# Scores one tile ahead of the softmax behind, and the last two row tiles of the down projection by halves of the tokens

## The chip, the cores and the metric

The kernel runs on one core of one Trainium2 chip. The time is the device time of one launch in microseconds; three runs of the kernel before were taken, and one more under the profiler.

## The reference, cut to what matters

Two layers over 512 tokens of width 1024 in float32. The first layer mixes tokens with a gated delta rule, the second with sliding-window attention; both also attend into 256 memory rows. After each mix comes a projection back to the width, and a feed-forward block. The change touches the attention of the second layer, and the end: the last down projection with the final norm.

```python
def sliding_window_attention(q, k, v, sinks):      # 12 heads of 64, window 128, blocks of 128 queries
    ...
    s = jnp.einsum("bnqhgd,bnkhd->bnhgqk", qb, kw).astype(jnp.float32) * (SWA_DH ** -0.5)
    ...
    m = jnp.maximum(jnp.max(s, axis=-1, keepdims=True), sink)
    p = jnp.exp(s - m)
    p = (p / (jnp.sum(p, axis=-1, keepdims=True) + jnp.exp(sink - m))).astype(v.dtype)
    o = jnp.einsum("bnhgqk,bnkhd->bnqhgd", p, vw)
...
for layer in range(DEPTH):
    ...
    x = x + jnp.concatenate([mix_out, mem_o], axis=-1) @ w_out[layer]
    x = x + swiglu(rms_norm(x, ln_ffn[layer]), w_gate_up[layer], w_down[layer])
    ...
return rms_norm(x, ln_final)
```

`memory_attention` is the same softmax attention without window and sinks, over 256 memory rows, 4 heads of 64.

## The kernel before, in words

Activations lie transposed: features on the 128 partitions, the 512 tokens along the free dimension, eight tiles `x[0..7]` for the width. Every large product is made of three matmuls (`mm3`): weight and activation are split into a high and a low part that TensorE takes at its fast rate, by `split` (ACT makes the high part `whi`, DVE the low part `wlo`), and high x high, high x low, low x high are added in PSUM. A projection (`project`) of one output tile is 8 x 3 = 24 matmuls of 128x512. Weights come by transfers from the SP queue into `wraw` (two buffers), and `whi` and `wlo` have three buffers each.

The program is written with a scheduler that takes the instructions in the order of the text as priority, and puts an instruction of lower priority ahead where its model of the times lets it start earlier. So the order on an engine isn't the order of the text alone. `nosync` adds an edge that only fixes the order of two instructions.

`swa` is the second layer's mixing. Eight attention tiles t: 0 to 5 hold two heads each of the window attention, 6 and 7 the memory heads. `queries(t)` projects tile t into `q` (three buffers) in a PSUM bank of the tag `pj` (two banks), and DVE applies the rotary embedding (`rope`, four operations). `attend(t)` calls `attention`, which does, for one tile of two heads and four blocks n of 128 queries: scores (TensorE, 8 matmuls into the double bank `qk`, twice: blocks 0 and 1, then 2 and 3, with one buffer); the masked maximum (DVE) into `sm`; exponentials with sums (ACT); the reciprocal and the scaling (DVE and ACT in turns); transposes of the probabilities into banks `pt` (two), their copies `pf`; products with the values into the bank `sc`; and the split of the result into `mix[t]`. `attention` serves the first layer's memory heads too. Then `output` projects, over mix tiles 6, 7, 0, 1, 2, 3, 4, 5, for each of eight output tiles.

`ffn` does the feed-forward block in two halves of 11 feature tiles. In the second half of the last layer, `tail` is 7: tiles 0 to 6 of the down projection are done with all 512 tokens, and tile 7 with the first 256 tokens and then the last 256. After each half of tile 7 comes `final`: the sum of squares by two matmuls with a matrix of ones, logarithm and exponential on ACT (`ps`, then a copy to `rstd`), products with the gains on DVE and, for tiles 4 and 5, on POOL, and four output transfers from SP.

Of the kernel before, what the change touches and what calls it, by code (L numbers as in the profile page):

```python
# [9 lines left out]
F32 = mybir.dt.float32  # L10
F32R = mybir.dt.float32r
I32 = mybir.dt.int32
AF = mybir.ActivationFunctionType
ALU = mybir.AluOpType
# [4 lines left out]
P = 128  # L19
T = 512  # L20
D = 1024
KD = D // P
# [63 lines left out]
class Builder:  # L86
# [53 lines left out]
        return self.nc.scalar.activation(out, in_, AF.Square).ins  # L140

    def mm(self, out, lhsT, rhs, start=True, stop=True):
        self.nc.tensor.matmul(out, lhsT, rhs, start=start, stop=stop)  # L143

    def tr(self, out, in_):
        k = in_.shape[0]
        self.nc.tensor.transpose(out, in_, self.ident[:k, :k])  # L147

    def tt(self, eng, out, a, b, op):
        return eng.tensor_tensor(out=out, in0=a, in1=b, op=op).ins  # L150
# [557 lines left out]


    def attention(self, pool, q, kk, vv, m, out, sinks=None):  # L710

        nc = self.nc
        win = sinks is not None
        own = "pt" in self.pbufs
        half = [slice(0, 64), slice(64, P)]
        sm = [self.t(pool, [P, 2, 2, 2 * P], F32, "sm", 4 if own else 2) for _ in range(2)]
        sm = [t[:, n] for t in sm for n in range(2)]
        mx = self.t(pool, [P, 2 * NC], F32, "mx", 2)
        den = self.t(pool, [P, 2 * NC], F32, "den", 2)
        nm = self.t(pool, [P, 2 * NC], F32, "nm", 2)  # L720
        for n0 in range(0, NC, 2):
            if own:
                two = self.bank("qk", [P, 2, 2, 2 * P])
                ps = [two[:, b] for b in range(2)]
            else:
                ps = [self.bank("sc" if n0 else "g", [P, 2, 2 * P]) for _ in range(2)]
            for n in (n0, n0 + 1):
                ks = slice((n - 1) * P if n else 0, (n + 1) * P) if win else slice(0, ML)
                c0 = P if win and n == 0 else 0
                for b in range(2):  # L730
                    self.mm(ps[b][:, n - n0, c0:], q[half[b], n * P:(n + 1) * P], kk[half[b], ks])
            for b in range(2):
                i = b * NC + n0
                if win:
                    for n in (n0, n0 + 1):
                        c0 = 0 if n else P
                        nc.vector.tensor_tensor_reduce(
                            out=sm[n][:, b, c0:], in0=ps[b][:, n - n0, c0:], in1=self.band[:, c0:], scale=1.0,
                            scalar=NEG, op0=ALU.add, op1=ALU.max, accum_out=mx[:, b * NC + n:b * NC + n + 1])
                else:  # L740
                    nc.vector.tensor_reduce(out=mx[:, i:i + 2], in_=ps[b], op=ALU.max, axis=AX.X)  # L741
                    self.ts(nm[:, i:i + 2], mx[:, i:i + 2], -0.125, ALU.mult)
                    for n in (n0, n0 + 1):
                        i = b * NC + n
                        self.fn(sm[n][:, b, :], ps[b][:, n - n0, :], AF.Exp, scale=0.125, bias=nm[:, i:i + 1],
                                accum_out=den[:, i:i + 1])
        if win:
            sk = sinks.unsqueeze(2).to_broadcast([P, 2, NC])
            v4 = lambda ap: ap.rearrange("p (b n) -> p b n", b=2)
            self.stt(v4(mx), v4(mx), 0.125, sk, ALU.mult, ALU.max)  # L750
            self.ts(nm, mx, -1.0, ALU.mult)
            es = self.t(pool, [P, 2 * NC], F32, "es", 2)
            self.tt(nc.vector, v4(es), v4(nm), sk, ALU.add)
            self.fn(es, es, AF.Exp)
            for n in range(NC):
                c0 = 0 if n else P
                for b in range(2):
                    i = b * NC + n
                    self.fn(sm[n][:, b, c0:], sm[n][:, b, c0:], AF.Exp, scale=0.125, bias=nm[:, i:i + 1],
                            accum_out=den[:, i:i + 1])  # L760
            self.tt(nc.vector, den, den, es, ALU.add)
        nc.vector.reciprocal(den, den)
        o = self.bank("sc")
        group = NC if own else 2
        for n in range(NC):
            if n % group == 0:
                pf = {}
            k0 = 1 if win and n == 0 else 0
            p = sm[n][:, :, k0 * P:]
            dn = den.rearrange("p (b n) -> p n b", b=2)[:, n, :]  # L770
            for b in range(2):
                if n % 2:
                    self.copy(p[:, b], p[:, b], scale=dn[:, b:b + 1])
                else:
                    self.ts(p[:, b], p[:, b], dn[:, b:b + 1], ALU.mult)
            pt = self.bank("pt" if own else "g", [P, 2, 2, P])
            for j in range(k0, 2):
                for b in range(2):
                    self.tr(pt[:, j, b, :], sm[n][:, b, j * P:(j + 1) * P])
            pf[n] = self.t(pool, [P, 2, 2, P], F32, "pf", group)  # L780
            if own and n == 2:
                nc.vector.tensor_copy(pf[n][:, k0:], pt[:, k0:])
            else:
                self.copy(pf[n][:, k0:], pt[:, k0:])
            if (n + 1) % group:
                continue
            for n, t in pf.items():
                for j in range(1 if win and n == 0 else 0, 2):
                    for b in range(2):
                        v = vv[n - 1 + j][:, half[b]] if win else vv[j][:, m * P + 64 * b:m * P + 64 * b + 64]  # L790
                        self.mm(o[half[b], n * P:(n + 1) * P], v, t[:, j, b, :], win and n == 0 or j == 0, j == 1)
        self.split(o, *out)


# [16 lines left out]
    def ffn(self, fp, xp, layer, h, apool, rope=False):  # L811
        nc, a = self.nc, self.a
        acc = self.acc
        half = FT // 2
        for f0 in (0, half):
# [16 lines left out]
                if rope and f == 4:  # L832
                    self.rope_tables(fp)
            self.acc = None
            tail = KD - 1 if f0 and layer else KD
            down = lambda m, j, n, **kw: self.weight(a["wdn"][layer, m][:, (f0 + j) * P:(f0 + j + n) * P], **kw)
            for m in range(tail):
                ps = self.bank("pj")
# [6 lines left out]
                    self.acc = self.accumulate(xp, self.acc, self.x[m], m)  # L845
        if tail < KD:

            w = {m: [down(m, j, n, pool=fp if m == KD - 1 and tail < KD - 1 else None) for j, n in ((0, 6), (6, 5))] for m in range(tail, KD)}
            for t in (slice(0, T // 2), slice(T // 2, T)):
                acc = self.acc[:, t]  # L850
                for m in range(tail, KD):
                    ps = self.bank("pj")[:, :T // 2]
                    for k in range(half):
                        self.mm3(ps, w[m][k // 6], k % 6, [x[:, t] for x in acts[k]], k == 0, k == half - 1)
                    x = self.x[m][:, t]
                    self.tt(nc.vector, x, ps, x, ALU.add)
                sq = self.t(fp, [P, T // 2], F32, "sql", 2)
                self.square(sq, x)
                self.final(fp, (acc, sq), t)

    def rstd_from(self, acc, t=slice(0, T)):
        self.use(LN_EXP)
# [50 lines left out]
    def swa(self, sp):  # L913
# [38 lines left out]
            self.copy(vt.rearrange("p c i -> p (c i)"), pt)  # L952
            vv.extend(vt[:, c, :] for c in range(NC))

        def attend(t):
            mix[t] = self.pair(self.bpool)
            if t < 6:
                self.attention(sp, qs[t], kk[0], vv, t, mix[t], sinks[:, t, :])
            else:
                self.attention(sp, qs[t], memK[t - 6], memV, t - 6, mix[t])  # L960

        queries(6)
        queries(7)
        keys()
        values()
        attend(6)
        transpose_values()
        queries(0)
        attend(7)
        for t in range(6):  # L970
            if t < 5:
                queries(t + 1)
            attend(t)
        return [mix[t] for t in range(KD)]

    def final(self, fp, squares, t):

        nc = self.nc
        self.use(LN_EXP)
        ps = self.bank("g")[:, t]  # L980
        for k, sq in enumerate(squares):
            self.mm(ps, self.ones, sq, k == 0, k == len(squares) - 1)
        self.fn(ps, ps, AF.Ln, scale=1.0 / D, bias=self.eps)
        self.fn(ps, ps, AF.Exp, scale=-0.5)
        r = self.rstd[:, t]
        self.copy(r, ps)
        rows = self.a["out"].rearrange("(k p) t -> p k t", p=P)
        for k0 in (4, 0, 2, 6):
            o = self.t(fp, [P, 2, T // 2], F32, f"fin{k0}", 2)
            for k in (k0, k0 + 1):  # L990
                x, y = self.x[k][:, t], o[:, k - k0, :]
                if k0 == 4:
                    self.copy(y, x, scale=self.gain(G_FIN, k))
                    self.tt(nc.gpsimd, y, y, r, ALU.mult)
                else:
                    self.stt(y, x, self.gain(G_FIN, k), ps, ALU.mult, ALU.mult)
            nc.sync.dma_start(rows[:, k0:k0 + 2, t], o)


def layout(i):  # L1000
# [56 lines left out]
```

## Time and profile before

| what | us |
|---|---|
| median of three runs (lowest, highest) | 1206.13 (1206.08, 1208.48) |
| the profiled execution | 1205.06 |
| its span, first to last instruction | 1203.3 |
| the second layer's attention, on the profile's time line | about 697 to 801 |
| the last row tile and the end | 1183.9 to 1203.3 |

The span is that of one execution; the 1.8 us between span and the execution's time lie around the program. The profile has, for each engine, the busy time; groups of equal instructions with their mean duration; the idle time in front of each and what ended it; and the instructions in order of time. PE is TensorE's matmuls, PEld its weight loads, DVE the vector engine, ACT the scalar engine, POOL GpSimd, SP the queue that issues the transfers.

### The profile page before, as it was taken

The numbers are of one execution on the slowest core, as the hardware profiler recorded it, in microseconds if no ns is written. First come the engines' busy times: TensorE is split into PE (matmuls) and PEld (weight loads), VectorE is DVE, ScalarE is ACT, GpSimd is POOL, SyncE is SP. The second block draws the span as 40 slices with busy tenths as digits, with TensorE's granted clock in tenths as the row PEclk, the third lists the DMA queues.
The fourth block names the chain that finished last, engine by engine and source line by source line (L and its number), as shares of the span: only waits on it lengthen the run. The fifth ranks groups of instructions, "written<-read, shape, count | busy, mean of one in ns | idle before, by whom it ended". The sixth has DMA issues, their size and how long they took to land.

```text
span 1203.3 us, 15347 instructions
## 1 busy us (share of the span) xinstructions
PE 1181.1 (98%) x6009; PEld 961.1 (80%) x6009; DVE 620.3 (52%) x1058; ACT 504.2 (42%) x929; POOL 92.5 (8%) x63
## 2 busy tenths in 40 slices
PE   7999999999999999999999999999999999999996
PEld 6888777877888888888888877678888888888885
DVE  5654977668753433343434667755434333444343
ACT  7578672456432322232333456664323222322332
POOL 0210000000011100011100000000111100111100
PEclk9999999999999999999999999999999999999999
DMA  7334352325323223423233411113232234232232
GB/s 297 134 95 130 95 129 79 121 77 162 105 88 105 84 84 96 123 88 105 84 84 97 139 54 42 47 37 122 88 105 88 82 96 120 89 104 89 84 97 81
DMA packets 51037, 121.08 MB, mean 101 GB/s; under 512 B 14300, under 2 KB 17012, under 8 KB 50964
## 3 DMA queue, kind: packets, MB, share of 16 engines
q1 hardware_dynamic: 50964, 120.10, 32.3%
q8 instruction: 47, 0.77, 0.3%
q14 instruction: 26, 0.21, 0.1%
HBM read 113.12 MB, written 6.96 MB: 100 GB/s over the span
## 4 chain that ended last, share of the span: by engine, by line
PE 89%; DVE 6%; ACT 2%; DMA 1%; issue 1%; SPq 0%; DVEq 0%; ACTq 0%
PE pj L143 57%; PE g L143 24%; PE sc L143 6%; DVE wlo L150 1%; PE pt L147 1%; ACT sm L131 1%; PE g L147 1%; DMA wraw<-in_wmk 1%; ACT whi L137 1%; DVE btmp L150 1%; PE qk L143 0%; DVE big L150 0%; DVE mx L741 0%; DMA wraw<-in_win 0%; DMA big<-basein 0%
## 5 line engine op out<-in xcount | busy, mean ns | idle before, releaser
L137 ACT ACTIVATE whi<-wraw 128x1024 fp32r<-128x1024 f32 (+2 forms) x213 | 207.6, 975 | 564.9 <-PE pj L143 366.6
L143 PE MATMUL pj<-h,whi 128*128 128x512 f32 (+1 forms) x972 | 381.6, 393 | 0.1
L143 PE MATMUL pj<-l,whi 128*128 128x512 f32 (+1 forms) x972 | 380.2, 391 | 0.0
L143 PE MATMUL pj<-h,wlo 128*128 128x512 f32 (+1 forms) x972 | 379.4, 391 | 0.0
L150 DVE TENSOR_TENSOR wlo<-wraw,whi 128x1024 fp32r<-128x1024 f32 (+2 forms) x213 | 238.3, 1119 | 147.0 <-ACT whi L137 146.6
L143 PEld LDWEIGHTS pj<-h,whi 128*128 128x128 f32 x972 | 182.5, 188 | 41.0 <-issue 4.2
L143 PEld LDWEIGHTS pj<-l,whi 128*128 128x128 f32 x972 | 182.7, 188 | 38.9 <-issue 2.6
L143 PEld LDWEIGHTS pj<-h,wlo 128*128 128x128 f32 x972 | 182.6, 188 | 38.9 <-issue 2.2
L150 POOL TENSOR_TENSOR fg<-fg,rstd 128x512 f32<-128x512 f32 x44 | 75.5, 1716 | 988.2 <-ACT fg L131 988.2
L143 PE MATMUL g<-h,wlo 128*128 128x512 f32 x380 | 148.0, 389 | 0.0
L143 PE MATMUL g<-l,whi 128*128 128x512 f32 x380 | 148.0, 389 | 0.0
L143 PE MATMUL g<-h,whi 128*128 128x512 f32 x380 | 147.9, 389 | 0.0
L150 DVE TENSOR_TENSOR fu<-g,fg 128x512 f32<-128x512 f32 x44 | 30.4, 691 | 142.7 <-PE g L143 140.0
L150 DVE TENSOR_TENSOR fg<-pj,rstd 128x512 f32<-128x512 f32 x44 | 30.4, 691 | 110.7 <-PE pj L143 110.4
L143 PEld LDWEIGHTS g<-h,wlo 128*128 128x128 f32 x380 | 71.4, 188 | 15.0 <-issue 0.2
L143 PEld LDWEIGHTS g<-h,whi 128*128 128x128 f32 x380 | 71.3, 188 | 14.8
L143 PEld LDWEIGHTS g<-l,whi 128*128 128x128 f32 x380 | 71.3, 188 | 14.8 <-issue 0.2
L150 DVE TENSOR_TENSOR x<-pj,x 128x512 f32<-128x512 f32 (+1 forms) x45 | 30.4, 678 | 68.2 <-PE pj L143 68.2
L131 ACT ACTIVATE fg<-fg 128x512 f32<-128x512 f32 x44 | 27.7, 630 | 1.5 <-DVE fg L150 1.5
L153 DVE SCALAR_TENSOR_TENSOR qv<-pj,gains,qv 128x511 f32<-128x511 f32 (+2 forms) x36 | 26.7, 743 | 1.1 <-ACT qv L137 0.8
L140 ACT ACTIVATE sq<-x 128x512 f32<-128x512 f32 x39 | 24.1, 624 | 6.2 <-DVE x L150 3.9
L137 ACT ACTIVATE h<-x,gains 128x512 fp32r<-128x512 f32 x32 | 22.1, 712 | 5.9 <-DVE x L150 5.9
(301 smaller groups left out, 1198.5 us busy)
## 6 DMA issues: line engine op xcount, KB each, us to landing
wraw<-in_wgu SPq DMA_DIRECT2D x88, 512.0 KB, 3.5
wraw<-in_win SPq DMA_DIRECT2D x26, 512.0 KB, 3.6
wraw<-in_wdn SPq DMA_DIRECT2D x32, 384.0 KB, 3.1
wraw<-in_wdn SPq DMA_DIRECT2D x32, 320.0 KB, 2.9
wraw<-in_wout SPq DMA_DIRECT2D x16, 512.0 KB, 3.5
wraw<-in_wq SPq DMA_DIRECT2D x8, 512.0 KB, 3.5
x<-in_xT SPq DMA_DIRECT2D x4, 512.0 KB, 9.0
wraw<-in_wmv SPq DMA_DIRECT2D x4, 512.0 KB, 9.0
```

Of the source, the lines that this page charges most:

```text
L131: ins = self.nc.scalar.activation(out, in_, func, **kw).ins
L137: self.copied = self.nc.scalar.activation(out, in_, AF.Copy, **kw).ins
L140: return self.nc.scalar.activation(out, in_, AF.Square).ins
L143: self.nc.tensor.matmul(out, lhsT, rhs, start=start, stop=stop)
L147: self.nc.tensor.transpose(out, in_, self.ident[:k, :k])
L150: return eng.tensor_tensor(out=out, in0=a, in1=b, op=op).ins
L153: self.nc.vector.scalar_tensor_tensor(out=out, in0=in0, scalar=scalar, in1=in1, op0=op0, op1=op1)
```

## The change

`attention` is cut in two: `scores` (up to the exponentials of the memory heads, or to the masked maximum of the window heads) and `weigh` (the rest). In `swa` the scores of tile t are written ahead of `weigh` of the tile before it. Two edges are added on TensorE: the first transpose of a tile's probabilities comes after the last score of the tile ahead, and the first value product after the last transpose of its group. The first layer still calls both in a row.

In the last feed-forward block `tail` becomes 6, so tiles 6 and 7 are both done by halves of the tokens, and the weights of tile 7 lie in another pool. The products of `x` with the final gain are made ahead on ACT for tiles 0 to 5, both halves. `final` now ends with two exponentials, one into PSUM and one into SBUF, and `store` multiplies: tiles 0 and 1 on POOL, 2 to 5 on DVE two at a time, 6 and 7 on DVE one at a time. The stores of both halves are written after both halves' matmuls. The diff, without the changes that only return an instruction:

```diff
@@ -708,9 +708,11 @@
 
 
     def attention(self, pool, q, kk, vv, m, out, sinks=None):
+        self.weigh(pool, self.scores(pool, q, kk, sinks is not None), vv, m, out, sinks)
+
+    def scores(self, pool, q, kk, win):
 
         nc = self.nc
-        win = sinks is not None
         own = "pt" in self.pbufs
         half = [slice(0, 64), slice(64, P)]
         sm = [self.t(pool, [P, 2, 2, 2 * P], F32, "sm", 4 if own else 2) for _ in range(2)]
@@ -728,7 +730,7 @@
                 ks = slice((n - 1) * P if n else 0, (n + 1) * P) if win else slice(0, ML)
                 c0 = P if win and n == 0 else 0
                 for b in range(2):
-                    self.mm(ps[b][:, n - n0, c0:], q[half[b], n * P:(n + 1) * P], kk[half[b], ks])
+                    self.scored = self.mm(ps[b][:, n - n0, c0:], q[half[b], n * P:(n + 1) * P], kk[half[b], ks])
             for b in range(2):
                 i = b * NC + n0
                 if win:
@@ -744,6 +746,15 @@
                         i = b * NC + n
                         self.fn(sm[n][:, b, :], ps[b][:, n - n0, :], AF.Exp, scale=0.125, bias=nm[:, i:i + 1],
                                 accum_out=den[:, i:i + 1])
+        return sm, mx, den, nm
+
+    def weigh(self, pool, scores, vv, m, out, sinks):
+
+        nc = self.nc
+        win = sinks is not None
+        own = "pt" in self.pbufs
+        half = [slice(0, 64), slice(64, P)]
+        sm, mx, den, nm = scores
         if win:
             sk = sinks.unsqueeze(2).to_broadcast([P, 2, NC])
             v4 = lambda ap: ap.rearrange("p (b n) -> p b n", b=2)
@@ -776,7 +787,11 @@
             pt = self.bank("pt" if own else "g", [P, 2, 2, P])
             for j in range(k0, 2):
                 for b in range(2):
-                    self.tr(pt[:, j, b, :], sm[n][:, b, j * P:(j + 1) * P])
+                    turned = self.tr(pt[:, j, b, :], sm[n][:, b, j * P:(j + 1) * P])
+                    if own and self.scored is not None:
+
+                        self.nosync(turned, self.scored)
+                        self.scored = None
             pf[n] = self.t(pool, [P, 2, 2, P], F32, "pf", group)
             if own and n == 2:
                 nc.vector.tensor_copy(pf[n][:, k0:], pt[:, k0:])
@@ -788,7 +803,10 @@
                 for j in range(1 if win and n == 0 else 0, 2):
                     for b in range(2):
                         v = vv[n - 1 + j][:, half[b]] if win else vv[j][:, m * P + 64 * b:m * P + 64 * b + 64]
-                        self.mm(o[half[b], n * P:(n + 1) * P], v, t[:, j, b, :], win and n == 0 or j == 0, j == 1)
+                        ins = self.mm(o[half[b], n * P:(n + 1) * P], v, t[:, j, b, :], win and n == 0 or j == 0, j == 1)
+                        if turned is not None:
+                            self.nosync(ins, turned)
+                            turned = None
         self.split(o, *out)
 
 
@@ -832,7 +850,7 @@
                 if rope and f == 4:
                     self.rope_tables(fp)
             self.acc = None
-            tail = KD - 1 if f0 and layer else KD
+            tail = KD - 2 if f0 and layer else KD
             down = lambda m, j, n, **kw: self.weight(a["wdn"][layer, m][:, (f0 + j) * P:(f0 + j + n) * P], **kw)
             for m in range(tail):
                 ps = self.bank("pj")
@@ -845,18 +863,30 @@
                     self.acc = self.accumulate(xp, self.acc, self.x[m], m)
         if tail < KD:
 
-            w = {m: [down(m, j, n, pool=fp if m == KD - 1 and tail < KD - 1 else None) for j, n in ((0, 6), (6, 5))] for m in range(tail, KD)}
-            for t in (slice(0, T // 2), slice(T // 2, T)):
+            parts = (slice(0, T // 2), slice(T // 2, T))
+            w = {m: [down(m, j, n, pool=fp if m == KD - 1 else None) for j, n in ((0, 6), (6, 5))] for m in range(tail, KD)}
+            outs = [self.t(fp, [P, KD, t.stop - t.start], F32, f"fin{t.start}") for t in parts]
+            for o, t in zip(outs, parts):
+                for k in range(tail):
+                    self.copy(o[:, k, :], self.x[k][:, t], scale=self.gain(G_FIN, k))
+            ends = []
+            for t in parts:
                 acc = self.acc[:, t]
                 for m in range(tail, KD):
-                    ps = self.bank("pj")[:, :T // 2]
+                    ps = self.bank("pj")[:, t]
                     for k in range(half):
                         self.mm3(ps, w[m][k // 6], k % 6, [x[:, t] for x in acts[k]], k == 0, k == half - 1)
                     x = self.x[m][:, t]
                     self.tt(nc.vector, x, ps, x, ALU.add)
-                sq = self.t(fp, [P, T // 2], F32, "sql", 2)
-                self.square(sq, x)
-                self.final(fp, (acc, sq), t)
+                    sq = self.t(fp, [P, T], F32, "sql", 2)[:, t]
+                    self.square(sq, x)
+                    if m < KD - 1:
+                        nxt = self.t(fp, [P, T], F32, "sqb", 2)[:, t]
+                        self.tt(nc.vector, nxt, acc, sq, ALU.add)
+                        acc = nxt
+                ends.append(self.final(fp, (acc, sq), t))
+            for (ps, r), o, t in zip(ends, outs, parts):
+                self.store(ps, r, o, t, tail)
 
     def rstd_from(self, acc, t=slice(0, T)):
         self.use(LN_EXP)
@@ -952,49 +982,62 @@
             self.copy(vt.rearrange("p c i -> p (c i)"), pt)
             vv.extend(vt[:, c, :] for c in range(NC))
 
-        def attend(t):
+        def score(t):
+            got[t] = self.scores(sp, qs[t], kk[0] if t < 6 else memK[t - 6], t < 6)
+
+        def weigh(t):
             mix[t] = self.pair(self.bpool)
             if t < 6:
-                self.attention(sp, qs[t], kk[0], vv, t, mix[t], sinks[:, t, :])
+                self.weigh(sp, got[t], vv, t, mix[t], sinks[:, t, :])
             else:
-                self.attention(sp, qs[t], memK[t - 6], memV, t - 6, mix[t])
-
+                self.weigh(sp, got[t], memV, t - 6, mix[t], None)
+
+        got = {}
         queries(6)
         queries(7)
         keys()
         values()
-        attend(6)
+        score(6)
         transpose_values()
         queries(0)
-        attend(7)
+        score(7)
+        weigh(6)
+        last = 7
         for t in range(6):
             if t < 5:
                 queries(t + 1)
-            attend(t)
+            score(t)
+            weigh(last)
+            last = t
+        weigh(last)
         return [mix[t] for t in range(KD)]
 
     def final(self, fp, squares, t):
 
-        nc = self.nc
         self.use(LN_EXP)
         ps = self.bank("g")[:, t]
         for k, sq in enumerate(squares):
             self.mm(ps, self.ones, sq, k == 0, k == len(squares) - 1)
-        self.fn(ps, ps, AF.Ln, scale=1.0 / D, bias=self.eps)
-        self.fn(ps, ps, AF.Exp, scale=-0.5)
-        r = self.rstd[:, t]
-        self.copy(r, ps)
+        l, r = (self.t(fp, [P, T], F32, n, 2)[:, t] for n in ("fl", "fr"))
+        self.fn(l, ps, AF.Ln, scale=1.0 / D, bias=self.eps)
+        self.fn(ps, l, AF.Exp, scale=-0.5)
+        self.fn(r, l, AF.Exp, scale=-0.5)
+        return ps, r
+
+    def store(self, ps, r, o, t, done):
+
+        nc = self.nc
         rows = self.a["out"].rearrange("(k p) t -> p k t", p=P)
-        for k0 in (4, 0, 2, 6):
-            o = self.t(fp, [P, 2, T // 2], F32, f"fin{k0}", 2)
-            for k in (k0, k0 + 1):
-                x, y = self.x[k][:, t], o[:, k - k0, :]
-                if k0 == 4:
-                    self.copy(y, x, scale=self.gain(G_FIN, k))
-                    self.tt(nc.gpsimd, y, y, r, ALU.mult)
-                else:
-                    self.stt(y, x, self.gain(G_FIN, k), ps, ALU.mult, ALU.mult)
-            nc.sync.dma_start(rows[:, k0:k0 + 2, t], o)
+        wide = lambda f, k: f.unsqueeze(1).to_broadcast([P, k, t.stop - t.start])
+        send = lambda a, b: nc.sync.dma_start(rows[:, a:b, t], o[:, a:b, :])
+        self.tt(nc.gpsimd, o[:, 0:2, :], o[:, 0:2, :], wide(r, 2), ALU.mult)
+        for k in range(2, done, 2):
+            self.tt(nc.vector, o[:, k:k + 2, :], o[:, k:k + 2, :], wide(ps, 2), ALU.mult)
+            send(k, k + 2)
+        for k in range(done, KD):
+            self.stt(o[:, k, :], self.x[k][:, t], self.gain(G_FIN, k), ps, ALU.mult, ALU.mult)
+        send(done, KD)
+        send(0, 2)
 
 
 def layout(i):
```

More of the change, by code (lines that the diff above doesn't have):

```diff
@@ L142, in mm @@
     def mm(self, out, lhsT, rhs, start=True, stop=True):
-        self.nc.tensor.matmul(out, lhsT, rhs, start=start, stop=stop)
+        return self.nc.tensor.matmul(out, lhsT, rhs, start=start, stop=stop).ins
     def tr(self, out, in_):
         k = in_.shape[0]
-        self.nc.tensor.transpose(out, in_, self.ident[:k, :k])
+        return self.nc.tensor.transpose(out, in_, self.ident[:k, :k]).ins
     def tt(self, eng, out, a, b, op):
```

## The prediction

> **What bounds the kernel now.** I read the page first, then the table by stage, then TensorE's instructions in order of time in the two places that the change touches.
>
> ```profile
> PE 1181.1 (98%) x6009; PEld 961.1 (80%) x6009; DVE 620.3 (52%) x1058; ACT 504.2 (42%) x929; POOL 92.5 (8%) x63
> PE 89%; DVE 6%; ACT 2%; DMA 1%; issue 1%; SPq 0%; DVEq 0%; ACTq 0%
> ```
>
> The first line is the busy time of each engine, the second the shares of the chain that ended last. TensorE (PE) is the bound: 98% of the span is busy and 89% of the chain is PE. So an edit can gain time in three ways only: fill PE's idle time, let it do the same work with fewer switches between kinds of matmul, or shorten what comes after its last matmul.
>
> ```profile
> core 0: us, PE busy (x) PEld busy (x) DVE busy (x) ACT busy (x) POOL busy (x), PEclk, DMA share, GB/s
> 697.20:800.70 103.50, 100.60 (x689) 72.91 (x688) 68.33 (x230) 68.44 (x206) 0.00 (x0) 1.00 0.13 41
> 743.70:755.50 11.80, 11.80 (x83) 8.45 (x82) 9.33 (x34) 6.80 (x20) 0.00 (x0) 1.00 0.15 47
> 755.50:768.40 12.90, 12.17 (x85) 8.70 (x84) 9.41 (x34) 11.18 (x39) 0.00 (x0) 1.00 0.16 42
> ```
>
> These are the stage in which the second layer attends (697.2 to 800.7), and two periods of it, one tile t each. PE idles 103.5 - 100.6 = 2.9 us in the whole stage, so that is all that hiding the softmax better can give. The two periods differ: one has no idle time, the next has 0.73 us, and ACT is busy 11.18 of 12.90 us there. DVE is busy 9.4 us of every tile. PE is ahead of them, but not by much.
>
> **What PE does in one such period.** Its instructions in order of time (start, duration, count; "pj" is projections, "qk" scores, "pt" transposes of the probabilities, "sc" probabilities times values):
>
> ```profile
> 755.53 0.93 PE L143 MATMUL qk<-ks,q 64*128 64x128 f32 x8
> 756.39 0.50 PE L143 MATMUL pj<-h,whi 128*128 128x512 f32 x1
> 756.73 0.39 PE L143 MATMUL pj<-l,whi 128*128 128x512 f32 x1
> ...
> 758.80 0.39 PE L143 MATMUL pj<-l,whi 128*128 128x512 f32 x1
> 759.02 0.39 PE L143 MATMUL pj<-h,wlo 128*128 128x512 f32 x1
> 759.34 1.13 PE L143 MATMUL qk<-ks,q 64*128 64x256 f32 x8
> 761.20 0.54 PE L147 MATMUL pt<-consts,sm 128*128 128x128 f32 x3 [0.73 <-DVE sm L157]
> 761.50 0.48 PE L143 MATMUL pj<-h,whi 128*128 128x512 f32 x1
> 761.82 0.96 PE L147 MATMUL pt<-consts,sm 128*128 128x128 f32 x7
> 762.71 0.44 PE L143 MATMUL sc<-pf,vt 128*64 128x128 f32 x4
> 763.08 0.50 PE L143 MATMUL pj<-l,whi 128*128 128x512 f32 x1
> 763.41 0.27 PE L147 MATMUL pt<-consts,sm 128*128 128x128 f32 x1
> 763.62 0.43 PE L143 MATMUL sc<-pf,vt 128*64 128x128 f32 x2
> 763.98 0.55 PE L147 MATMUL pt<-consts,sm 128*128 128x128 f32 x3
> 764.46 1.52 PE L143 MATMUL sc<-pf,vt 128*64 128x128 f32 x22
> 765.91 0.50 PE L143 MATMUL pj<-h,wlo 128*128 128x512 f32 x1
> ```
>
> Starts are what to read, since matmuls overlap. Projections follow each other at 0.22 to 0.23 us (758.80 to 759.02). A projection in front of another kind is followed 0.32 us later (759.02 to 759.34), and the first projection after another kind takes 0.34 us (756.39 to 756.73). So an excursion from projections and back costs about 0.2 us on top of its own matmuls. And the scheduler has already put all scores of the tile ahead in front of the transposes here (both qk groups precede the pt): the transposes wait 0.73 us because the softmax behind them ended late, and then they and the value matmuls are cut into seven pieces.
>
> **Part 1: scores ahead, each kind in one piece.** Nothing is removed or added on any engine: the same 16 scores, 14 transposes and 28 value matmuls per tile (16, 16, 32 for the two memory tiles), the same DVE and ACT instructions, no DMA. What changes is the order. Each tile's scores come before the weighing of the tile behind, the first transpose of that tile is held on PE's queue behind the last score, and the first value matmul behind the last transpose.
>
> The switches. From the first pt to the next projection after the sc, 761.20 to 765.91, this tile takes 4.71 us with 2 projections inside. In one piece it would be: 14 transposes at 0.11 us (seven start-to-starts in 762.71 - 761.82 = 0.89, some of which is the switch) = 1.6, 28 value matmuls at 0.065 us (22 in 765.91 - 764.46 = 1.45) = 1.8, two projections at 0.23, and 0.2 for one excursion = 4.1. That is 0.6 us. Two more rows with a wait in front of the transposes, and the projection that follows the second's value matmuls:
>
> ```profile
> 737.85 0.54 PE L147 MATMUL pt<-consts,sm 128*128 128x128 f32 x3 [0.40 <-DVE sm L157]
> 784.53 0.54 PE L147 MATMUL pt<-consts,sm 128*128 128x128 f32 x3 [0.71 <-DVE sm L157]
> 789.24 0.50 PE L143 MATMUL pj<-l,whi 128*128 128x512 f32 x1
> ```
>
> 784.53 to 789.24 is 4.71 us again. Four of the six tiles with a window are cut in this manner; the other two are cut less, for which I allow 0.4, and the two memory tiles, in pieces of eight transposes and 32 value matmuls, give nothing: 4 x 0.6 + 2 x 0.4 = 3.2 us at most. Two banks for pt mean that the third and fourth group of transposes still wait for the copy of the first, so some projections will still stand between. I take half, 1.6 us; the ends are 0 and 3.2.
>
> The idle time. The rows of the groups that carry it:
>
> ```profile
> L147 PE MATMUL pt<-consts,sm 128*128 128x128 f32 x116 | 17.9, 282 | 2.4 <-DVE sm L157 2.3
> L143 PE MATMUL qk<-mk,q 64*128 64x256 f32 x32 | 4.5, 402 | 0.5 <-ACT sm L131 0.5
> ```
>
> 2.4 us is transposes waiting for scaled probabilities. In the new order the softmax of a tile has from its last score to the last score of the next tile, a whole period of some 11 us. Its own work is eight reductions, of which four come before the last score, eight exponentials and eight scalings on two engines; at the 0.37 us that a 128x256 activation takes in a row below, that is (4 + 8 + 4) x 0.37 = 6 us in a row, so the wait should go. The 0.5 us of the memory scores waits for a score bank, of which there is still one pair, and stays. I take 2.2 of the 2.9; the ends are 0 and 2.9, and a loss is the second rival. What is late next is PE's own work.
>
> What is queued behind the new order: on PE, the held transposes have the value matmuls and mix[t] behind them, and then nothing but the output projection, which takes mix 6, 7, 0 to 5 in that order; projections of the next queries fill the holds as long as a bank of pj (two) and a buffer of q (three) are free. DVE and ACT get the score reductions of tile t in front of the scalings of t-1. No queue of SP or POOL is passed. Part 1: 3.8 us gained.
>
> **Part 2: two row tiles of the down projection by halves.** The end of the profile:
>
> ```profile
> 1176.36 0.39 PE L143 MATMUL pj<-h,whi 128*128 128x512 f32 x1
> 1183.92 0.28 PE L143 MATMUL pj<-h,whi 128*128 128x256 f32 x1
> 1187.87 0.60 PE L143 MATMUL g<-sqa,consts 128*128 128x256 f32 x2
> 1188.07 0.42 DVE L150 TENSOR_TENSOR x<-pj,x 128x256 f32<-128x256 f32 x1 [1.81 <-PE pj L143]
> 1192.76 0.28 PE L143 MATMUL pj<-ac10h,wlo 128*128 128x256 f32 x1
> 1191.09 2.44 DVE L153 SCALAR_TENSOR_TENSOR fin<-x,gains,g 128x256 f32<-128x256 f32 x6 [2.60 <-ACT rstd L137]
> 1193.45 0.42 DVE L150 TENSOR_TENSOR x<-pj,x 128x256 f32<-128x256 f32 x1
> 1195.59 0.37 ACT L131 ACTIVATE g<-g 128x256 f32<-128x256 f32 x1
> 1195.99 0.38 ACT L137 ACTIVATE rstd<-g 128x256 f32<-128x256 f32 x1
> 1196.40 2.44 DVE L153 SCALAR_TENSOR_TENSOR fin<-x,gains,g 128x256 f32<-128x256 f32 x6 [2.54 <-ACT rstd L137]
> 1198.87 1.00 SPq L997 DMA_DIRECT2D out_dram<-fin  x2
> ```
>
> It adds PE time: tile 6 in one piece takes 1183.92 - 1176.36 = 7.56 us for 33 matmuls; half of tile 7 takes 1187.87 - 1183.92 = 3.95 us for 33 of half width. Two halves are 7.90: +0.34 us, all on the path. The Trainium skill (TensorE: Matmul & The Clock Gate, section "Back-to-back issue gap") gives 518 cycles for 512 columns and 262 for 256; by it the split would cost 33 x 6 cycles, an estimate of 0.08 us instead of 0.34. The rows decide, and I keep 0.34.
>
> It frees the second half's residual add. It could start 0.32 us after the last matmul's start (as in the first half: 1188.07, where the last one starts 0.12 us before 1187.87), at 1193.08; it starts at 1193.45, behind the six products of the first half. With two tiles per half the first half's chain ends four us before: -0.37 us, hidden under 7.9 us of matmuls.
>
> It shortens the end. Call E the end of the second exponential, 1195.96. Now a copy to rstd follows, DVE starts at E + 0.44, and of the last two output transfers, issued from 1198.87 to 1199.87, the second is issued half-way, at E + 3.4. After: the copy becomes a second exponential from SBUF that DVE doesn't wait for. DVE does two products of 128x512 and two of 128x256. For the wide ones I take 0.69 us:
>
> ```profile
> L150 DVE TENSOR_TENSOR x<-pj,x 128x512 f32<-128x512 f32 (+1 forms) x45 | 30.4, 678 | 68.2 <-PE pj L143 68.2
> L150 POOL TENSOR_TENSOR DT<-gcr,consts 128x512 f32<-128x512 f32 x6 | 8.5, 1452 | 10.6 <-DMA gcr<-dr 10.6
> ```
>
> The first reads one PSUM operand too, though not a repeated one; no row shows that. So DVE is done at E + 2.2, not 2.9; POOL, with a repeated operand at 1.45 us (second row), at E + 0.4 + 1.5 = 1.9. SP issues (6,8) at E + 2.2 and (0,2) half a microsecond later: E + 2.7 instead of 3.4, -0.7 us. If a repeated PSUM operand took twice as long, this would be a loss of 0.6. The twelve scaled copies on ACT (0.38 us each, as the copy to rstd, 4.6 in all) lie under the down projections, two for each 7.6 us of matmuls, on an engine that is busy 42% of the span; without that cover they would sit in front of the squares. The weights of tile 7 move to a pool of their own, so no buffer is waited for. Part 2: 0.34 - 0.37 - 0.7 = -0.7, between -1.2 and +0.6.
>
> **Sum.** 3.8 + 0.7 = 4.5 us off. The profiled execution took 1205.06 us (span 1203.3 and 1.8 around it); the median of the runs shown is 1206.13, 1.1 above it. So 1200.6 for a profiled execution like this one, 1201.6 for the median.
>
> **Rivals.** *Nothing left to hide.* The rows above already show both score groups ahead of the transposes in this tile; a scheduler that moves projections into every hole may give the new order the same number of pieces and a new wait of the same size, for the copies between the transposes. For it: the period from 743.70 has no idle time at all. Against it: three of the eight tiles wait 0.4 us or more, and four are cut in seven pieces. Then part 1 gives 0 to 1.5, part 2 its 0.7: about 1204.6. Chance 0.17.
>
> *The holds become waits.* The transposes can't start before the second score group, and that group needs the score bank, which DVE frees after four reductions; if the four rotary operations and a weight split (at 0.69 us for 128x512: 2.8 and 1.4 us, and 1.4 for the reductions) stand on DVE, the bank is free some 5.6 us after the first group. That is just what 24 projections fill (24 x 0.225 = 5.4 us). Program order puts those in front of the scores, so the fill may be used up, with only two pj banks to go on. From there PE waits at the head of the transposes: with 1.5 us in each of six tiles, 9 us, less the 3.8 and 0.7: 1210.6. For it: DVE is busy 9.4 us in every tile, ACT up to 11.2. Against: q has three buffers, so the next projection may start before. Chance 0.18.
>
> *All of it comes.* All idle time gone, all pieces joined, part 2 at its best: 2.9 + 3.2 + 1.2 = 7.3, 1198.8; this is the low end of the forecast's own range.
>
> **How the numbers follow.** Forecast 0.65 (1198.8 to 1203.7), nothing left 0.17 (1203.7 to 1206), waits 0.18 (over 1206, centre 1210.6). The range takes in the forecast and the second case and the near part of the third, where holds cost less than the gains: 1198.5 to 1207.5, leaving out some 0.14 above and 0.05 below. 0.2% is 2.4 us, about what a measurement of this kernel can tell from no change. Faster by more than that (under 1203.7) 0.64, same (to 1208.5) 0.20, slower 0.16.
>
> **What the changed profile would show.** Right: in the attention stage idle before pt near 0 instead of 2.4; 14 transposes in one or two pieces, 28 value matmuls in one; the stage 3 to 4 us shorter; at the end a residual add 0.3 us after the last matmul, no wait of DVE for rstd, and 7.9 us where 7.56 were. Wrong: idle time on PE before pt with DVE or ACT as releaser in every tile; as many pieces as now; DVE products of 128x512 well over 0.7 us; a stage before or after the attention that changed.

## The result, and the profile after

The changed kernel took 1201.18 us (median of six runs, 1200.07 to 1203.6), the kernel before 1206.11 in the same comparison: ratio 0.9959, 95% interval 0.9945 to 0.9973. The forecast was 1201.6. The sum came out, but two of its terms missed in opposite directions: that the total is so near is in part luck, and most of what follows is about that.

The page of the changed kernel, the lines that answer to those shown of before:

```profile
PE 1178.0 (98%) x6042; PEld 962.2 (80%) x6042; DVE 620.2 (52%) x1056; ACT 507.0 (42%) x938; POOL 92.3 (8%) x61
...
PE 91%; DVE 5%; ACT 2%; DMA 1%; issue 0%; SPq 0%; DVEq 0%; ACTq 0%
```

TensorE is still the bound, busy 3.1 us less. Its 33 further matmuls are the halved row tile.

To compare kernels I cut the time line at events that all of them share. Stage A runs from the first memory score to the last residual add of the second output projection; stage B from the residual add of row tile 5 in the last down projection to the end of the span. Between A and B lie 346.06 us in each of these traces (346.07 in one). The table by stage, for before (A, B) and after (A, B); the columns are stretch, length, busy time of PE, PEld, DVE, ACT and POOL with the number of instructions, then the granted TensorE clock, the busy share of the DMA engines and GB/s:

```profile
697.75:830.50 132.75, 129.85 (x818) 97.23 (x818) 89.52 (x258) 84.03 (x228) 0.00 (x0) 1.00 0.18 58
1176.56:1203.28 26.72, 17.61 (x107) 15.20 (x105) 10.10 (x20) 6.70 (x14) 2.84 (x4) 0.92 0.25 83
```

```profile
697.56:827.26 129.70, 126.87 (x818) 97.13 (x818) 89.60 (x257) 83.62 (x228) 0.00 (x0) 1.00 0.19 60
1173.32:1198.80 25.48, 17.87 (x140) 16.80 (x138) 8.81 (x17) 6.12 (x14) 2.57 (x2) 0.92 0.26 87
```

A is 3.05 us shorter and B 1.24: with the 0.19 us by which A starts earlier, that is the whole 4.48 us between the spans (1203.28 and 1198.80). In A, length less PE's busy time is the idle time: 2.90 before, 2.83 after. So nearly all of A's gain is busy time, with the same 818 matmuls recorded and a granted clock of 1.00 in both. The groups with idle time in A, changed kernel:

```profile
L147 PE MATMUL pt<-consts,sm 128*128 128x128 f32 x116 | 18.4, 282 | 2.1 <-DVE sm L157 2.0
L143 PE MATMUL qk<-mk,q 64*128 64x256 f32 x32 | 4.5, 402 | 0.5 <-ACT sm L131 0.5
```

The wait before the transposes, 2.4 us before, is still 2.1. What did change is seen in the period that answers to the one quoted in the prediction (the projections between the two groups of scores left out):

```profile
755.02 0.93 PE L143 MATMUL qk<-ks,q 64*128 64x128 f32 x8
...
759.32 1.14 PE L143 MATMUL qk<-ks,q 64*128 64x256 f32 x8
760.66 1.14 PE L147 MATMUL pt<-consts,sm 128*128 128x128 f32 x6 [0.21 <-DVE sm L157]
761.55 0.48 PE L143 MATMUL pj<-h,wlo 128*128 128x512 f32 x1
761.87 0.39 PE L143 MATMUL pj<-h,whi 128*128 128x512 f32 x1
762.10 0.71 PE L147 MATMUL pt<-consts,sm 128*128 128x128 f32 x5
762.57 0.47 PE L143 MATMUL pj<-l,whi 128*128 128x512 f32 x1
762.88 0.55 PE L147 MATMUL pt<-consts,sm 128*128 128x128 f32 x3
763.36 1.75 PE L143 MATMUL sc<-pf,vt 128*64 128x128 f32 x28
765.04 0.50 PE L143 MATMUL pj<-h,wlo 128*128 128x512 f32 x1
```

The value products are one piece of 28; the transposes are still three. (A piece is a run of matmuls of one kind with no other kind between.) From the first transpose to the projection behind the value products it took 4.38 us (760.66 to 765.04) with three projections inside, where 4.71 us with two stood before. Over the stage the order of the program has 86 pieces instead of 93 on TensorE; those of value products fell from 18 to 9, those of transposes stayed (25 and 26), and so did those of projections (31 and 32).

### The profile page after: what moved, and what is told of

Read it like the earlier page. It is cut to its first block, busy times and chain, and to the rows that moved or that the text cites. A ratio compares the mean times of both kernels' runs of the same rounds, so it can differ in the third digit from the quotient of the medians.

```text
span 1198.8 us, 15416 instructions
## 1 busy us (share of the span) xinstructions
PE 1178.0 (98%) x6042; PEld 962.2 (80%) x6042; DVE 620.2 (52%) x1056; ACT 507.0 (42%) x938; POOL 92.3 (8%) x61
## 4 chain that ended last, share of the span: by engine, by line
PE 91%; DVE 5%; ACT 2%; DMA 1%; issue 0%; SPq 0%; DVEq 0%; ACTq 0%
PE pj L143 59%; PE g L143 24%; PE sc L143 6%; PE pt L147 1%; DVE wlo L150 1%; PE g L147 1%; ACT sm L131 1%; DMA wraw<-in_wmk 1%; DVE btmp L150 1%; DVE big L150 0%; DVE sm L739 0%; DMA big<-basein 0%; PE qk L143 0%; DVE q L150 0%; ACT whi L137 0%
```

## The experiments

All start from the changed kernel unless said otherwise. Their times are medians of 4 to 11 executions, of one where it is said; the comparison by stages is sharper, as the last section shows.

**One part alone.** Each of the two parts was put on the kernel before by itself.

> Part 1 alone: the attention of the changed kernel with the end of the kernel before. Stage A, from the first memory score to the last residual add of the second output projection, is 132.75 us before and 129.70 changed; stage B, from the residual add of row tile 5 in the last down projection to the end of the span, is 26.72 and 25.48. Theory: the two parts add up, A 129.7, B 26.7, median 1203.0. Rival: part of the gain needs both, A above 130.5 or B off 26.7 by more than 0.3.

> Part 2 alone: the end of the changed kernel with the attention of the kernel before. Theory: A 132.75, B 25.5, median 1204.9. Rival: B near 26.4, as the product of the forecast's terms without the faster landing (26.72 - 0.7 = 26.0) or less.

Part 1 alone took 1202.63 us (ratio to before 0.9975, 0.9965 to 0.9985), part 2 alone 1204.42 (0.9987, 0.9978 to 0.9996). Stage A, then B, of part 1 alone, and the same of part 2 alone:

```profile
696.26:825.88 129.62, 126.77 (x818) 97.16 (x818) 89.69 (x258) 83.60 (x228) 0.00 (x0) 1.00 0.19 59
1171.94:1198.65 26.71, 17.61 (x107) 15.20 (x105) 10.10 (x20) 6.70 (x14) 2.84 (x4) 0.90 0.25 82
```

```profile
698.47:831.24 132.77, 129.88 (x818) 97.19 (x818) 89.64 (x257) 84.02 (x228) 0.00 (x0) 1.00 0.18 58
1177.30:1202.80 25.50, 17.86 (x140) 16.80 (x138) 8.81 (x17) 6.12 (x14) 2.57 (x2) 0.91 0.26 88
```

The parts add up to within 0.1 us in each stage; the rivals fall.

**Which piece of part 1.** Part 1 is an order of the text and two edges. They were taken away one at a time.

```diff
-                        if turned is not None:
-                            self.nosync(ins, turned)
-                            turned = None
```

> Changed kernel without the second edge: a tile's first value product is no longer held behind its last transpose. TensorE's pieces in the attention rise from 86 to 94, those of value products from 9 to 18 as before the change. Theory (what was gained are the joined value products): A back to 132 to 132.7. Rival (what was gained is the order of the text, scores ahead of the softmax behind): A stays near 129.7 to 130.2.

Measured 1203.68 us; A 132.45. Without the second edge, nearly all of part 1 is gone (2.75 of 3.05). Then the second edge with the old order of the text:

```diff
         score(6)
+        weigh(6)
         transpose_values()
         queries(0)
         score(7)
-        weigh(6)
-        last = 7
+        weigh(7)
         for t in range(6):
             if t < 5:
                 queries(t + 1)
             score(t)
-            weigh(last)
-            last = t
-        weigh(last)
+            weigh(t)
```

> Changed kernel with the old order of the text (each tile's scores followed by its own weighing) and no first edge, but with the second edge: 89 pieces, 10 of them value products. Theory (joined value products): A 129.7 to 130.5, nearly all of the gain without the reordering. Rival (order of the text): A near 132.7, or longer, as the held products wait with nothing to hide them.

Measured 1202.70 us; A 130.77: 1.98 of 3.05 us with nothing but the value products joined. The theory had 129.7 to 130.5 and missed by 0.27, as the order of the text with the first edge is worth some more: 1.07 us beside the second edge, 0.3 without it.

> Changed kernel without the first edge: the first transpose may come before the last score of the tile ahead. 82 pieces instead of 86 (11 value pieces instead of 9, 28 of projections instead of 32). Theory (pieces of value products): A within 0.4 of 129.70, since the second edge is still there. Rival (the first edge carries the gain): A above 131.

> Changed kernel without both edges, only the order of the text changed: 95 pieces, 19 of value products. Theory: A 132.3 to 133. Rival (the order of the text alone hides softmax): A under 131.5.

Without the first edge 1201.09 us and A 130.10; without both A 131.96 (one run, 1202.87). So the first edge is worth 0.4 us when the second is there, and costs 0.5 when it isn't (132.45 against 131.96). For the run without both edges the theory had 132.3 to 133; 131.96 lies just below it, the rival (under 131.5) falls, and the order of the text alone gave 0.8.

The other way round, the same products in more pieces:

```diff
-        group = NC if own else 2
+        group = 1 if own else 2
-            pf[n] = self.t(pool, [P, 2, 2, P], F32, "pf", group)
+            pf[n] = self.t(pool, [P, 2, 2, P], F32, "pf", NC if own else 2)
```

> Changed kernel in which the value products of each block of queries follow that block's own transposes (groups of one block instead of four): 25 or 26 value pieces in the order instead of 9, the same matmuls. Theory (each further value piece costs 0.31 us, as 9 more cost 2.9 between the changed kernel and the one before, idle taken off): A less TensorE's idle there 126.98 + 16 x 0.31 = 132 us. Rival (the gain belongs to the order of the scores, the pieces only go with it): A less idle under 129.

It took 1203.92 us (one run). Stage A of this kernel, of the one without the second edge, of the old order with it, of the one without the first edge, and of the one without both, in this order:

```profile
698.48:830.57 132.09, 130.57 (x818) 96.69 (x818) 89.81 (x258) 84.01 (x228) 0.00 (x0) 1.00 0.18 58
```

```profile
699.85:832.30 132.45, 129.92 (x818) 97.84 (x818) 89.72 (x258) 83.58 (x228) 0.00 (x0) 1.00 0.18 58
```

```profile
700.00:830.77 130.77, 127.94 (x818) 96.44 (x818) 89.60 (x257) 83.89 (x228) 0.00 (x0) 1.00 0.19 59
```

```profile
697.97:828.07 130.10, 127.45 (x818) 97.72 (x818) 89.31 (x257) 83.22 (x228) 0.00 (x0) 1.00 0.18 59
```

```profile
697.59:829.55 131.96, 129.63 (x818) 97.81 (x818) 89.26 (x257) 83.87 (x228) 0.00 (x0) 1.00 0.19 58
```

PE's busy time against the number of value pieces: 9 pieces 126.87 (changed), 10 pieces 127.94, 11 pieces 127.45, 18 pieces 129.85 (before) and 129.92, 19 pieces 129.63, 25 pieces 130.57. It rises with them, by 0.2 to 0.3 us a piece over the whole, and not with the count of all pieces: 82 pieces without the first edge, 86 in the changed kernel, and the former is 0.6 us busier. The line isn't exact: 10 pieces cost more than 11, and from 18 to 25 it rises by 0.1 us a piece only. For 25 pieces the 0.31 us a piece of the expectation was too much: 132 was expected (from 126.98, where the table has 126.87) and 130.57 came, 0.23 a piece. The rival, under 129, falls.

The starts of single matmuls in stage A of the kernels before and after tell why the kind of a piece matters. Transposes cut by projections, in the changed kernel:

```profile
737.36 0.27 PE L147 MATMUL pt<-consts,sm 128*128 128x128 f32 x1
737.38 0.48 PE L143 MATMUL pj<-h,whi 128*128 128x512 f32 x1
737.70 0.49 PE L147 MATMUL pt<-consts,sm 128*128 128x128 f32 x3
```

The projection starts 0.02 us after the transpose and the next transpose 0.32 us later: 0.34 for the two. Uncut they take as much, 0.11 for a transpose followed by another and 0.23 for a projection followed by another. So a cut of this kind costs nothing. A value product within its piece is followed after 0.06 us on average, the last one of a piece after 0.20 us, whatever the next kind is; and a transpose is followed by a value product after 0.20 us instead of 0.11. That makes 0.23 us for a value piece between transposes, and about 0.1 more where a projection comes behind it.

**Why the transposes still wait.** In the prediction the softmax was to have a whole period to itself. DVE and ACT of the changed kernel around the wait at 749 us (some rows left out):

```profile
744.80 1.06 ACT L137 ACTIVATE whi<-wraw 128x1024 fp32r<-128x1024 f32 x1
748.79 1.31 ACT L137 ACTIVATE sm<-sm,den 128x256 f32<-128x256 f32 x3 [2.93 <-DVE den L773]
```

```profile
747.28 0.17 DVE L150 TENSOR_TENSOR den<-den,es 128x8 f32<-128x8 f32 x1
747.36 1.23 DVE L150 TENSOR_TENSOR wlo<-wraw,whi 128x1024 fp32r<-128x1024 f32 x1
748.49 0.20 DVE L773 RECIPROCAL den<-den 128x8 f32<-128x8 f32 x1
748.73 0.75 DVE L157 TENSOR_SCALAR sm<-sm,den 128x128 f32<-128x128 f32 x3
```

ACT has done its exponentials before the weight split at 744.80 and then stands idle for 2.93 us, until the reciprocal. On DVE the two operations that make it, 0.4 us of work, stand behind rotary operations, the score reductions of the next tile (the last of them starts at 746.93) and a weight split. In the kernel before, the reductions and the split stood ahead of the reciprocal too, but the exponentials ended only just before it (ACT, then DVE, at its wait of 0.73 us):

```profile
759.71 0.49 ACT L131 ACTIVATE sm<-sm,nm 128x256 f32<-128x256 f32 x1
759.18 1.22 DVE L150 TENSOR_TENSOR wlo<-wraw,whi 128x1024 fp32r<-128x1024 f32 x1
760.53 0.20 DVE L762 RECIPROCAL den<-den 128x8 f32<-128x8 f32 x1
```

So the change gave the exponentials time, and left the reciprocal where it was. The waits at 749, 761 and 772 us (0.50, 0.21 and 0.57) have this pattern: a place in a queue, not the length of the softmax. The longest, 0.70 at 737 us, hasn't: there DVE waits for the exponentials. So the next kernel writes the normalisation of the tile behind ahead of the next scores:

```diff
             if t < 5:
                 queries(t + 1)
+            norm(last)
             score(t)
-            weigh(last)
+            turn(last)
```

`norm` is the part of `weigh` up to the reciprocal (exponentials, sums), `turn` the scaling, the transposes and the value products.

> Changed kernel with weigh cut in two: the exponentials and the reciprocal of the tile behind are written ahead of the scores of the next tile, transposes and value products stay behind them; both edges stay. 75 pieces instead of 86. Theory (the 2.0 us that TensorE still idles before transposes, and most of the single projections between them, come from a reciprocal that stands late on DVE's queue behind the next tile's score reductions): idle before transposes under 1, A 126.5 to 128.5. Rival (the wait is the length of the softmax itself): idle stays near 2, A near 129.7 or longer, as the scores are now late.

It took 1199.83 us (0.9952 of before, 0.9939 to 0.9964). Its stage A, its waiting group, the same place on the time line, and DVE ahead of the wait that was at 737 us:

```profile
697.97:826.55 128.58, 126.63 (x818) 97.23 (x818) 88.96 (x258) 84.09 (x228) 0.00 (x0) 1.00 0.19 60
```

```profile
L147 PE MATMUL pt<-consts,sm 128*128 128x128 f32 x116 | 17.7, 281 | 1.1 <-DVE sm L157 0.7 <-ACT pf L137 0.3
```

```profile
746.84 0.20 DVE L777 RECIPROCAL den<-den 128x8 f32<-128x8 f32 x1
...
748.73 1.22 DVE L150 TENSOR_TENSOR wlo<-wraw,whi 128x1024 fp32r<-128x1024 f32 x1
```

```profile
749.21 1.57 PE L147 MATMUL pt<-consts,sm 128*128 128x128 f32 x10
...
750.85 0.60 PE L147 MATMUL pt<-consts,sm 128*128 128x128 f32 x4
751.38 1.75 PE L143 MATMUL sc<-pf,vt 128*64 128x128 f32 x28
```

```profile
736.50 0.17 DVE L150 TENSOR_TENSOR den<-den,es 128x8 f32<-128x8 f32 x1 [1.64 <-ACT sm L131]
```

A is 1.12 us shorter, of which 0.9 is idle time. The reciprocal now comes ahead of the weight split, the transposes follow the scores without a wait, in pieces of ten and four. The three waits of this pattern are gone. Idle before transposes is 1.1 us where the theory had under 1, and A lies a little above its 126.5 to 128.5: the wait at 737 us stays (0.67), as DVE stands idle there for 1.64 us until ACT's exponentials end, and a new one of 0.28 waits for a copy of the transposes. The rival (idle near 2) falls for three of the four waits, and holds for the longest.

**The end.** Only row tile 7 by halves, as before, with the new products and stores:

```diff
-            tail = KD - 2 if f0 and layer else KD
+            tail = KD - 1 if f0 and layer else KD
...
-                for k in range(tail):
+                for k in range(KD - 2):
...
-                self.store(ps, r, o, t, tail)
+                self.store(ps, r, o, t, KD - 2)
```

> Changed kernel with only row tile 7 by halves, as before, but with the new end (products with the gain made ahead, second exponential instead of the copy, wide products). Theory (the end's own chain carries part 2, halving tile 6 gives 0.37 - 0.26 = 0.1): B 25.6, against 25.48 and 26.72. Rival (the longer cover carries it): B 26.2 or more, as the first half's products again stand in front of the second half's residual add.

Measured 1200.91 us. Its stage B, and DVE at the end of the first half and the start of the second's residual add:

```profile
1175.32:1200.48 25.16, 17.55 (x107) 15.15 (x105) 8.48 (x15) 5.92 (x13) 2.57 (x2) 0.93 0.26 88
```

```profile
1190.57 0.87 DVE L153 SCALAR_TENSOR_TENSOR fin<-x,gains,g 128x256 f32<-128x256 f32 x2
1191.78 0.42 DVE L150 TENSOR_TENSOR x<-pj,x 128x256 f32<-128x256 f32 x1 [0.34 <-PE pj L143]
```

B is 25.16: shorter by 0.32 us than the changed kernel's 25.48, and the residual add waits for TensorE, not for the first half's products. The theory's 25.6 missed: it had halving row tile 6 gain 0.1 us, and halving it gains nothing and costs the matmuls' price, 0.32. The whole gain at the end is the end's own chain.

**Together.**

> The two edits that were faster than the changed kernel together: the normalisation of the tile behind ahead of the next scores, and only row tile 7 by halves with the new end. Theory: the stages add, A 128.6, B 25.2, so 1.4 us under the changed kernel. Rival: run to run spread of the first 698 us hides it in the median; then the stages still show it.

> The kernel before this one in the list without the first edge: 70 pieces, 10 of value products. Theory (value pieces and idle decide, the first edge buys one value piece less): A 128.6 to 129.0. Rival (all pieces cost alike): A 127.8 or less, with 5 pieces fewer.

Stage A of the two:

```profile
697.31:825.90 128.59, 126.62 (x818) 97.26 (x818) 89.02 (x258) 83.94 (x228) 0.00 (x0) 1.00 0.18 60
```

```profile
698.15:827.10 128.95, 127.20 (x818) 97.69 (x818) 88.52 (x257) 83.98 (x228) 0.00 (x0) 1.00 0.19 60
```

The first took 1199.46 us (0.9946 of before, 0.9933 to 0.9960), with A 128.59 and B 25.14: by the stages it beats both kernels, and lies 1.45 us under the changed one. Without the first edge 1200.10, A 128.95: five pieces fewer and 0.36 us longer, so again not all pieces cost alike.

## Why the prediction was right, and where not

**Idle time: the step that failed.** "So the wait should go", 2.2 us taken. It went down from 2.90 to 2.83 for all of A. The time for the softmax was counted as work in a row, with nothing in front of it on DVE; in three of the four waits its reciprocal stands in DVE's queue behind the next tile's reductions and a weight split, as it did before the change in the period shown. The prediction named that ("score reductions of tile t in front of the scalings of t-1") and gave it no price; moving the two operations ahead took 1.0 us off the wait. In the fourth the exponentials themselves are late.

**Switches: the mechanism right, the size too small.** 1.6 us was taken, half of the 3.2 that was worked out as the most; 2.98 came (129.85 to 126.87 busy). The reason for taking half was that transposes would still be cut by projections. They are, but that costs nothing: the 0.2 us for an excursion from projections was read where scores stand between, and doesn't hold for transposes. So in the period shown nearly all of the 0.6 us that one piece of each kind was to give came with the transposes in three pieces: 4.71 to 4.38 us, with 0.23 for the further projection taken off. The gain sits in the value products, whose 9 further pieces go with 2.98 us, 0.3 each. The two misses, 2.1 too much and 1.4 too little, left 3.05 where 3.8 was said. Of the signs that the prediction listed, the value products in one piece and the shorter stage came; the idle time near 0 and the transposes in one or two pieces did not.

**The end.** +0.34 for the halves: the runs show 0.32. The residual add is no longer late, -0.37, but the cover that the prediction named for it, two tiles per half, isn't what does it: with one tile per half the add isn't late either, since the new chain leaves DVE free in time. From E, the end of the second exponential, the last transfer was to be issued at E + 2.7:

```profile
1192.27 0.39 ACT L131 ACTIVATE g<-fl 128x256 f32<-128x256 f32 x1
1192.59 0.40 ACT L131 ACTIVATE fr<-fl 128x256 f32<-128x256 f32 x1
1192.68 1.28 DVE L150 TENSOR_TENSOR fin<-fin,g 128x512 f32<-128x512 f32 x2 [2.17 <-ACT g L131]
1193.06 1.27 POOL L150 TENSOR_TENSOR fin<-fin,fr 128x512 f32<-128x512 f32 x1 [7.61 <-ACT fr L131]
1195.25 0.45 SPq L1032 DMA_DIRECT2D out_dram<-fin  x1
```

1195.25 is E + 2.6. DVE starts 0.02 us after E and doesn't wait for the second exponential, and a repeated PSUM operand costs no more than the 0.69 us that the prediction took from plain ones (1.28 us for two). From the end of the last issue to the end of the span it took 3.10 us (1195.70 to 1198.80) instead of 3.41 (1199.87 to 1203.28), 0.31 us that no term had; why it is shorter was not looked into. So part 2 gave 1.24 us, just past the good end of its bounds (1.2), where 0.7 was the sum.

**The rivals.** "Nothing left to hide" was right about the idle time and wrong about what followed: the same idle time, and still 3 us from the pieces. "The holds become waits" didn't come: of the idle time before the transposes no tile has more than 0.70 us. On the price of 256 columns: by the section "Back-to-back issue gap" of TensorE: Matmul & The Clock Gate in the Trainium skill the halves would cost an estimated 0.08 us; the trace disagrees, with 0.32.

## What to carry to other kernels

Where TensorE is busy 98% of the time, count how often it changes kind, and which kind is cut: here, joining short value products by one order-only edge was worth more than hiding the softmax, and two thirds of it (1.98 of 3.05 us) could be had without moving anything, while transposes cut by projections cost nothing. A price of a switch read between two kinds need not hold for two others. When a wait is to be hidden by writing other work ahead of it, look at what that work does to the queue of the engine that ends the wait; the two short operations that make the reciprocal had to be written ahead as well. When a forecast comes out, check its terms by themselves: two of these were off by 1.4 and 2.1 us in opposite directions, and part 2 made up by luck most of what they lacked.

## What the runs showed that I had not expected

The start of stage A, which no edit here touches on TensorE, lies between 696.26 and 700.00 us in these traces, a spread of 3.7 us, while A and B repeat to 0.1 us in kernels with the same order. Between the two extremes the difference is made in three places: 1.8 us in the first 20 us, 1.1 at about 62 and 0.7 at about 139 us. In the first, ACT waits for the transfers of the memory rows 5.0 us in one and 2.8 in the other; at the other two TensorE waits for another engine, 0.91 us against none and 2.34 against 1.61. What makes the waits differ was not traced. So medians of kernels that differ by 1 us say little here, and stages cut at common events say much.
